# Layer 1's value rows in seven buffers, gate reads tied to a tile six ahead, and the last norm's weights read near the end

## The chip, the cores and the metric

The kernel runs on one core of one Trainium2 chip. The metric is the device time of one execution, in microseconds (us). It is given as a median of several executions, and separately for one profiled execution, whose trace is what is read below. A TensorE matmul is written PE, its weight load PEld; DVE is VectorE, ACT is ScalarE, POOL is GpSimd, SP is SyncE. SP, ACT and POOL also issue the transfers (DMA); "ACTq" and "SPq" in a row mean that issuing side.

## The reference

Two layers are applied to 256 tokens of width 1024 (and, in layer 0 alone, to 256 context tokens). Each layer has a mixer (a convolution, a neighbourhood attention and a grouped attention) and then a feed-forward part with 16384 experts (PEER). The change touches the feed-forward part:

```python
q = (xc @ w_q).reshape(PEER_CHUNK, PEER_HEADS, 2, PEER_D_KEY)
s = jnp.einsum('chpk,hpnk->chpn', q, sub_keys).astype(jnp.float32)
top_s, top_i = lax.top_k(s, PEER_TOPK)
...
g = jax.nn.softmax(best_s, axis=-1).astype(xc.dtype)
act = jax.nn.gelu(jnp.einsum('cd,chkd->chk', xc, jnp.take(u, idx, axis=0)))
return jnp.einsum('chk,chkd->cd', g * act, jnp.take(v, idx, axis=0))
```

Each token picks 16 experts for each of 8 heads; `u` and `v` hold one row of 1024 numbers per expert. At the very end the tokens go through one more root-mean-square norm with the weights `final_norm_g`.

## The kernel before

Most tokens are not gathered but computed against all experts. The 16384 experts of a layer are 128 tiles of 128. For a tile `e` the activations of its experts for all dense tokens are one product with `u` (helper `act`, the matmul of layer 1 is L630, those of layer 0 go through L119 to L121), they are multiplied by a gate that is zero for experts that a token did not pick (L827), and the result is multiplied with the tile's value rows `v` and summed in PSUM over all tiles (`down_proj`: L119 to L121 with the value rows split into a high and a low half, and in layer 1 also L842 on the unsplit rows). A few tokens go the other way: their rows are gathered with indirect transfers (L926) and worked on by DVE (L914, L921). These gathers are spread over the tiles by `gather_steps`.

`route` works out the gates and writes them to DRAM (`gd`), 128 x 128 x 16 numbers for each group of 16 tokens. `sweep` then goes over the tiles in order. It reads gates for 8 tiles at a time into `gr` (two buffers, transfers issued by ACT, L825); in layer 1 the gates of tiles 0 to 7 never leave the chip (`near`). 32 activation tiles of layer 1 (42 of layer 0) are computed while `route` still runs and are kept in DRAM (`spilled`); the sweep reads them back in pairs (`gback`, L719, issued by ACT). 8 more in layer 1 (4 in layer 0) wait in buffers. So in layer 1 the sweep's first 40 tiles need no new activations, while later ones need one 512 KB read of `u` and one of `v` per tile, both issued by SP (L109). `u` has a ring of three buffers (`rawu`), and so has `v` (`rawv`). A value buffer is free again when ACT has made the high half (L97), DVE the low half (L99) and PE has done its products with the raw rows (L842).

The order of the instructions on each engine is fixed before the run, by a planner that goes by a model of times, by data and buffers, and by the edges that `hold` adds (the first argument may not start before the second has ended). On the chip each engine, and each issuing queue, works strictly in that order. The list `los` holds, for each tile, the DVE instruction that ends the preparation of its gated activations (L832). Tiles are prepared up to two ahead of PE, since `whi` and `wlo` have two buffers.

In layer 1 the buffers `hiu` and `lou` (two each, 4 KB per partition, as large as a value tile) hold the split halves of the query weights before the sweep; the sweep itself does not use them, because layer 1 multiplies with unsplit `u`.

Of the kernel before, what the change touches and what calls it, by code (L numbers as in the profile page):

```python
# [11 lines left out]
F32 = mybir.dt.float32  # L12
# [9 lines left out]
P = 128  # L22
T = 256
D = 1024
# [17 lines left out]
NE = 128  # L42
EG = 8
GA = {0: 4, 1: 8}
SPILL = {0: 42, 1: 32}
GLAG = 3
GB = 8
WOV = {0: (0, 1), 1: (1, 1)}
ZAT = (0, 2, 4, 6, 7, 9)
# [3 lines left out]
def hymba_kernel(ctx: ExitStack, tc: tile.TileContext, a, out):  # L53
    nc = tc.nc
# [4 lines left out]
    ring = ctx.enter_context(tc.tile_pool(name="ring", bufs=2))  # L59
# [3 lines left out]
    def bank(tag, nm):  # L63
        return psum.tile([P, 512], F32, tag=tag, name=nm)
# [21 lines left out]
    def hold(ins, after):  # L86

        if after is not None:
            tc.add_manual_dep(ins.ins, after.ins.name,
                              mybir.DependencyInfo(mybir.DependencyClass.Sync, mybir.DependencyReason.DATA),  # L90
                              reason="work that would crowd out more urgent work")


    def split(raw, shape, kind, nm, lo_eng=None, after=None):
        hi = ring.tile(shape, F32R, tag="hi" + kind, name="hi_" + nm)
        lo = ring.tile(shape, F32R, tag="lo" + kind, name="lo_" + nm)
        S.activation(hi, raw, AF.Copy)  # L97
        if lo_eng is None or lo_eng is V:
            V.tensor_tensor(lo, raw, hi.bitcast(F32), ALU.subtract)  # L99
        else:  # L100
            n = shape[1] // 4 if len(shape) == 3 and shape[1] == NC else 0
            for i in range(4):
                sl = (slice(None), slice(i * n, (i + 1) * n)) if n else (slice(None), i // 2, slice((i % 2) * 256, (i % 2 + 1) * 256))
                hold(lo_eng.tensor_tensor(lo[sl], raw[sl], hi[sl].bitcast(F32), ALU.subtract), after)  # L104
        return hi, lo

    def load(src, shape, kind, nm):
        raw = ring.tile(shape, F32, tag="raw" + kind, name="raw_" + nm, bufs=3)
        nc.sync.dma_start(raw, src)  # L109
        return raw  # L110
# [479 lines left out]
    def peer(l):  # L590
# [120 lines left out]
        def act_of(e, sw, after):  # L711
# [5 lines left out]
            if i % 2 == 0:  # L717
                two[0] = sw.tile([P, 2, nd], F32, tag="gback", name=f"gback{l}_{e}", bufs=GB // 2)
                hold(nc.scalar.dma_start(two[0], spilled[:, i:i + 2, :]), after)  # L719
# [89 lines left out]
    def sweep(l, dense, gath, act, h2n, eidx, gates, gd, nd, nb):  # L809
        sw = ctx_peer.enter_context(tc.tile_pool(name=f"sw{l}", bufs=2))  # L810
        pair = l == DEPTH - 1
        nw = P if pair else nd
        acc = [[bank(f"x{j}", f"acc{l}{j}{h}") for h in range(1 if pair and j else 2)] for j in range(len(dense))]
        steps = gather_steps(l, gath or [1], h2n, eidx, gates, sw, H if pair else P)
        ng = len(steps)
        ahead = GA[l] + SPILL[l]
        gr = None
        rows = None
        last = []
        los = []  # L820
        for e in range(NE):
            ga = act(e, sw, los[(e - GA[l]) // 2] if 0 <= e - GA[l] < GB else None)
            if e % EG == 0 and e >= NEAR[l]:
                gr = sw.tile([P, nb, EG, TB], F32, tag="gr", name=f"gr{l}_{e}")
                nc.scalar.dma_start(gr, gd[1][:, :, e:e + EG, :])  # L825
            g = gr[:, :, e % EG, :] if e >= NEAR[l] else gd[0][:, :, e, :]
            wi = V.tensor_tensor(ga[:, :nd].rearrange("p (b t) -> p b t", t=TB),  # L827
                            ga[:, :nd].rearrange("p (b t) -> p b t", t=TB), g, ALU.mult)
            whi = sw.tile([P, nw], F32R, tag="whi", name=f"whi{l}_{e}")
            wlo = sw.tile([P, nw], F32R, tag="wlo", name=f"wlo{l}_{e}")  # L830
            S.activation(whi, ga[:, :nw], AF.Copy)  # L831
            los.append(V.tensor_tensor(wlo, ga[:, :nw], whi.bitcast(F32), ALU.subtract))  # L832
            if e >= 2:
                hold(wi, los[e - 2])
            raw = load(a["v"][l, e], [P, D], "v", f"v{l}_{e}")
            v = split(raw, [P, D], "v", f"v{l}_{e}")

            def down_proj(j, h, e=e, whi=whi, wlo=wlo, v=v, ga=ga, raw=raw):
                ts, hs = slice(j * P, (j + 1) * P), slice(h * 512, (h + 1) * 512)
                if pair and j:  # L840

                    return [PE.matmul(acc[1][0][k * H:(k + 1) * H], lhsT=ga[:, P:P + H], rhs=raw[:, k * 512:(k + 1) * 512],  # L842
                                      start=e == 0, stop=e == NE - 1) for k in range(2)]
                return mm3(acc[j][h], whi[:, ts], wlo[:, ts], v[0][:, hs], v[1][:, hs], e == 0, e == NE - 1)

            if e < NE - 2:
                for j in range(len(dense)):
                    for h in range(len(acc[j])):
                        down_proj(j, h)
            else:  # L850
                last.append(down_proj)
            while steps and (e >= NE - 2 or ng - len(steps) < ng * (4 * e - 3 * min(e, ahead)) // (480 - 3 * ahead)):
                steps.pop(0)(wi)
            if e == NE - 12:
                rows = gate_rows(l, 5, [0, 1] if gath else [0], "mm")
            if e == NE - 2 and not pair:
                for g, t in enumerate(gath):
                    V.tensor_tensor(h2n[g], h2n[g], rows[t // 2], ALU.mult)
                    V.tensor_tensor(resid[t], resid[t], h2n[g], ALU.add)
                    for h in range(2):  # L860
                        squares(t, h)
        assert not steps
        if l == DEPTH - 1:
            fg = sw.tile([P, D], F32, name="fg", bufs=1)
            nc.scalar.dma_start(fg, a["fin_g"].partition_broadcast(P))
            V.tensor_scalar(fg, fg, 32.0, None, op0=ALU.mult)

        prev = None
        for j, h, e in LORD[l]:
            if e is None:  # L870

                accs = sw.tile([P, 512], F32, tag="ap", name="accs", bufs=3)
                S.activation(accs, acc[1][0], AF.Copy)
                acc[1] = [bank("x2", f"accj{k}") for k in range(2)]
                ins = []
                for k in range(2):
                    ins += [PE.matmul(acc[1][k][:H], lhsT=ident[:, k * H:(k + 1) * H], rhs=accs, start=True, stop=True),
                            PE.matmul(acc[1][k][H:], lhsT=fold, rhs=h2n[0][:, k * 512:(k + 1) * 512], start=True, stop=True)]
            else:
                ins = last[e](j, h)  # L880
            for i in ins:
                hold(i, prev)
                prev = i
        for j, t in [(1, 1), (0, 0)] if pair else enumerate(dense):
            for h in range(2):
                residual(sw, t, h, acc[j][h], rows, norm_ins["h10"][0] if len(dense) == 3 and j == 2 else None)
            if len(dense) == 3 and j == 1:
                norm_rs["h10"] = inv_rms(cst, [0, 1], "h10")
            if l == DEPTH - 1:
                y = sw.tile([P, D], F32, tag="grow", name=f"y{t}", bufs=GLAG + 1)  # L890
                y = [y[:, :512], y[:, 512:]]
                G.tensor_tensor(y[1], resid[t][:, 512:], fg[:, 512:], ALU.mult)
                rs = inv_rms(sw, [t], f"f{t}")
                V.scalar_tensor_tensor(y[0], resid[t][:, :512], rs, fg[:, :512], op0=ALU.mult, op1=ALU.mult)
                S.activation(y[1], y[1], AF.Copy, scale=rs)
                for h in range(2):
                    nc.sync.dma_start(out[t * P:(t + 1) * P, h * 512:(h + 1) * 512], y[h])

    def gather_steps(l, gath, h2n, eidx, gates, sw, ns):
# [5 lines left out]
        def use(after):  # L905
            rows, f = waiting.pop(0)
            hold(f(rows), after)

        for g in range(len(gath)):
# [13 lines left out]
            def step(k, after, g=g, t=t, down=down, up=up):  # L923
                s = k % ns
                r = sw.tile([P, D], F32, tag="grow", name=f"gr{'uv'[k // ns]}{l}{t}{s}", bufs=GLAG + 1)
                d = G.indirect_dma_start(out=r, out_offset=None, in_=a["v_rows" if k >= ns else "u_rows"],  # L926
                                         in_offset=bass.IndirectOffsetOnAxis(ap=eidx[g][:, s:s + 1], axis=0))
                hold(d, after)
                waiting.append((r, lambda rows, s=s, f=up if k >= ns else down: f(s, rows)))
                if len(waiting) > GLAG:  # L930
                    use(after)
# [3 lines left out]
        if steps:  # L935
            steps.extend([use] * GLAG)
        return steps
# [89 lines left out]
```

## Time and profile before

| | us |
|---|---|
| median of 3 executions | 2615.96 (2612.59 to 2622.68) |
| the profiled execution | 2629.2 |
| its span in the trace | 2627.1 |
| PE busy in the span | 2491.1 (95%) |
| DVE busy | 1831.6 (70%) |
| ACT busy | 1052.3 (40%) |
| POOL busy | 1050.9 (40%) |

The trace begins with the span; 2.1 us of the profiled execution lie outside of it. A matmul counts as busy while it is in the pipeline, so PE's share says little about its pace; the pace is read from the times between starts. "Granted clock" is the share of TensorE's full clock that it was given: of its two levels, 1.0 stands for 2.4 GHz and 0.5 for 1.2 GHz, and a value between is a mean over a stretch. The sweep of layer 0 begins at about 700 us of the span, that of layer 1 at about 2008 us, and the last tile of layer 1 ends at about 2612 us.

### The profile page before, as it was taken

The numbers are of one execution on the slowest core, as the hardware profiler recorded it, in microseconds if no ns is written. First come the engines' busy times: TensorE is split into PE (matmuls) and PEld (weight loads), VectorE is DVE, ScalarE is ACT, GpSimd is POOL, SyncE is SP. The second block draws the span as 40 slices with busy tenths as digits, with TensorE's granted clock in tenths as the row PEclk, the third lists the DMA queues.
The fourth block names the chain that finished last, engine by engine and source line by source line (L and its number), as shares of the span: only waits on it lengthen the run. The fifth ranks groups of instructions, "written<-read, shape, count | busy, mean of one in ns | idle before, by whom it ended". The sixth has DMA issues, their size and how long they took to land. (4 is left out here: it accounts for less than half of the span.)

```text
span 2627.1 us, 38186 instructions
## 1 busy us (share of the span) xinstructions
PE 2491.1 (95%) x13837; PEld 2023.0 (77%) x13837; DVE 1831.6 (70%) x3506; ACT 1052.3 (40%) x1708; POOL 1050.9 (40%) x967
## 2 busy tenths in 40 slices
PE   7999999888899999999999998998998999999997
PEld 4755788877898888989989987855997756777775
DVE  1754589989546677787888885374994467666667
ACT  3345633367533333333333334445454333323323
POOL 3713434768642244454545441722600114223222
PEclk9999999999999999999999999998999999999999
DMA  7343364356878889999999992441579889999996
GB/s 270 104 169 122 127 245 145 119 211 263 311 257 276 293 295 328 326 343 339 347 331 342 338 336 85 161 164 49 159 241 344 278 286 326 377 356 361 350 366 234
DMA packets 263565, 681.42 MB, mean 259 GB/s; under 512 B 23840, under 2 KB 112976, under 8 KB 260304
## 3 DMA queue, kind: packets, MB, share of 16 engines
q1 hardware_dynamic: 121712, 423.48, 45.4%
q0 software_dynamic: 55296, 201.35, 20.8%
q10 hardware_dynamic: 86368, 54.15, 7.2%
q8 instruction: 109, 1.79, 0.3%
q14 instruction: 80, 0.66, 0.1%
HBM read 628.63 MB, written 49.44 MB: 258 GB/s over the span
## 5 line engine op out<-in xcount | busy, mean ns | idle before, releaser
L120 PE MATMUL acc<-lo_v,whi 128*128 128x512 f32 x1024 | 406.1, 397 | 2.9 <-DVE lo_v L99 2.8
L99 DVE TENSOR_TENSOR lo_v<-raw_v,hi_v 128x1024 fp32r<-128x1024 f32 x256 | 313.5, 1225 | 119.9 <-ACT hi_v L97 119.1
L630 PE MATMUL psu<-h2raw,raw_u 128*128 128x192 f32 x2048 | 364.9, 330 | 10.1 <-DMA raw_u<-in_u 6.3
L121 PE MATMUL acc<-hi_v,wlo 128*128 128x512 f32 x1024 | 374.4, 392 | 0.0
L97 ACT ACTIVATE hi_v<-raw_v 128x1024 fp32r<-128x1024 f32 x256 | 269.1, 1052 | 260.4 <-PE acc L121 234.5
L630 PEld LDWEIGHTS psu<-h2raw,raw_u 128*128 128x128 f32 x2048 | 339.8, 191 | 40.2 <-issue 20.7
L121 PE MATMUL psu<-ahi_m,lo_u 128*128 128x384 f32 x1024 | 351.7, 343 | 10.2 <-DVE lo_u L99 6.6
L119 PE MATMUL psu<-ahi_m,hi_u 128*128 128x384 f32 x1024 | 349.9, 342 | 7.0 <-ACT hi_u L97 2.9
L120 PE MATMUL psu<-alo_m,hi_u 128*128 128x384 f32 x1024 | 349.8, 342 | 0.0
L119 PE MATMUL acc<-hi_v,whi 128*128 128x512 f32 x1024 | 346.2, 404 | 2.9 <-ACT hi_v L97 2.7
L926 POOL DMA_INDIRECT gru<-in_u_rows,eidx x128 | 183.6, 1435 | 286.3 <-DVE gback L827 144.8
L119 PEld LDWEIGHTS acc<-hi_v,whi 128*128 128x128 f32 x1024 | 184.9, 188 | 104.1 <-ACT gact L633 55.2
L921 DVE SCALAR_TENSOR_TENSOR h2n<-grv,dots,h2n 128x1024 f32<-128x1024 f32 x190 | 243.0, 1279 | 26.0 <-DMA grv<-in_v,eidx 24.6
L914 DVE SCALAR_TENSOR_TENSOR gru<-gru,h2n 128x1024 f32<-128x1024 f32 x192 | 232.0, 1220 | 36.7 <-DMA gru<-in_u_rows,eidx 31.8
L104 POOL TENSOR_TENSOR lo_u<-raw_u,hi_u 128x256 fp32r<-128x256 f32 x184 | 213.1, 1190 | 95.2 <-ACT hi_u L97 84.0
L926 POOL DMA_INDIRECT grv<-in_v,eidx x128 | 171.3, 1338 | 188.3 <-DVE h2n L921 164.3
L926 POOL DMA_INDIRECT gru<-in_u_rows,egl x64 | 90.2, 1409 | 376.3 <-DMA spilled<-gsp 123.2
L120 PEld LDWEIGHTS acc<-lo_v,whi 128*128 128x128 f32 x1024 | 192.6, 188 | 55.8 <-issue 5.7
L121 PEld LDWEIGHTS acc<-hi_v,wlo 128*128 128x128 f32 x1024 | 192.3, 188 | 38.1 <-DVE wlo L832 0.3
L831 ACT ACTIVATE whi<-gact 128x128 fp32r<-128x128 f32 (+1 forms) x182 | 74.6, 410 | 337.2 <-PE acc L120 189.8
L121 PEld LDWEIGHTS psu<-ahi_m,lo_u 128*128 128x128 f32 x1024 | 195.7, 191 | 16.9 <-DVE lo_u L99 8.6
L119 PEld LDWEIGHTS psu<-ahi_m,hi_u 128*128 128x128 f32 x1024 | 195.8, 191 | 13.1 <-ACT gsp L633 3.5
(287 smaller groups left out, 4581.3 us busy)
## 6 DMA issues: line engine op xcount, KB each, us to landing
raw_u<-in_u SPq DMA_DIRECT2D x256, 512.0 KB, 5.6
raw_v<-in_v SPq DMA_DIRECT2D x256, 512.0 KB, 6.0
ada<-in_ada SPq DMA_DIRECT2D x96, 512.0 KB, 4.7
gd<-stage SPq DMA_DIRECT2D x24, 1024.0 KB, 5.5
gr<-gd ACTq DMA_DIRECT2D x16, 1536.0 KB, 25.2
raw_wq<-in_w_q SPq DMA_DIRECT2D x32, 512.0 KB, 3.6
raw_wout<-in_w_out SPq DMA_DIRECT2D x24, 512.0 KB, 3.5
gd<-stage SPq DMA_DIRECT2D x12, 960.0 KB, 5.8
```

The source lines that it names most:

```text
L97: S.activation(hi, raw, AF.Copy)
L99: V.tensor_tensor(lo, raw, hi.bitcast(F32), ALU.subtract)
L104: hold(lo_eng.tensor_tensor(lo[sl], raw[sl], hi[sl].bitcast(F32), ALU.subtract), after)
L119: return [PE.matmul(o, lhsT=ahi, rhs=bhi, start=first, stop=False), PE.matmul(o, lhsT=ahi, rhs=blo, start=False, stop=False), PE.matmul(o, ...
L120: PE.matmul(o, lhsT=ahi, rhs=blo, start=False, stop=False),
L121: PE.matmul(o, lhsT=alo, rhs=bhi, start=False, stop=last)]
L630: PE.matmul(ps[:, :nd], lhsT=u[:, c, :], rhs=h2raw[:, c, :nd], start=c == 0, stop=c == NC - 1)
L831: S.activation(whi, ga[:, :nw], AF.Copy)
L914: return V.scalar_tensor_tensor(r, r, 1.0, h2n[g], op0=ALU.mult, op1=ALU.mult, accum_out=dots[:, s:s + 1])
L921: return V.scalar_tensor_tensor(h2n[g], r, dots[:, s:s + 1], h2n[g], op0=ALU.mult, op1=ALU.add)
L926: d = G.indirect_dma_start(out=r, out_offset=None, in_=a["v_rows" if k >= ns else "u_rows"], in_offset=bass.IndirectOffsetOnAxis(ap=eidx[g ...
```

## The change

There are three edits, all in `sweep`.

```diff
+GRL = 6
+VRING = (("hiu", 2), ("lou", 2), ("rawv", 3), ("hiu", 2), ("lou", 2), ("rawv", 3), ("rawv", 3))
...
                 gr = sw.tile([P, nb, EG, TB], F32, tag="gr", name=f"gr{l}_{e}")
-                nc.scalar.dma_start(gr, gd[1][:, :, e:e + EG, :])
+                hold(nc.scalar.dma_start(gr, gd[1][:, :, e:e + EG, :]), los[e - GRL] if e >= GRL else None)
...
-            raw = load(a["v"][l, e], [P, D], "v", f"v{l}_{e}")
+            if pair:
+
+                tag, bufs = VRING[e % len(VRING)]
+                raw = ring.tile([P, D], F32, tag=tag, name=f"raw_v{l}_{e}", bufs=bufs)
+                nc.sync.dma_start(raw, a["v"][l, e])
+            else:
+                raw = load(a["v"][l, e], [P, D], "v", f"v{l}_{e}")
...
             fg = sw.tile([P, D], F32, name="fg", bufs=1)
-            nc.scalar.dma_start(fg, a["fin_g"].partition_broadcast(P))
+            hold(nc.scalar.dma_start(fg, a["fin_g"].partition_broadcast(P)), los[NE - 16])
```

In layer 1 (`pair`) the value rows of seven tiles in a row now go into seven buffers: two `hiu`, two `lou` and three `rawv`. In both layers the gate read of a block of 8 tiles that begins at tile `e` may start only when the gated activations of tile `e - 6` are ready; before, it could start as soon as one of the two `gr` buffers was free, that is, when the last gates of the block two earlier had been used (tile `e - 9`), and the first two reads at once. The read of the final norm's weights (512 KB in SBUF) may start only when the activations of tile 112 of layer 1 are ready. No instruction of arithmetic is added or removed, and the same bytes are read.

## Rows read from the trace of the kernel before

**Rows 1.** Stages of layer 1's sweep: from and to, length, then busy us of PE, PEld, DVE, ACT and POOL (number of instructions), granted clock, share of the DMA engines' time, GB/s. All in us from the span's start.

```profile
2008.00:2140.00 132.00, 128.99 (x589) 86.95 (x588) 57.23 (x99) 40.95 (x74) 16.44 (x10) 0.97 0.87 290
2140.00:2182.00 42.00, 36.28 (x141) 18.30 (x140) 32.28 (x54) 17.54 (x29) 12.79 (x7) 0.96 0.86 294
2182.00:2240.00 58.00, 56.21 (x269) 40.01 (x268) 40.32 (x70) 17.95 (x33) 26.56 (x17) 1.00 0.93 340
2240.00:2560.00 320.00, 320.00 (x1606) 240.35 (x1606) 212.91 (x304) 99.07 (x188) 95.92 (x82) 1.00 0.98 361
2588.00:2610.00 22.00, 20.60 (x86) 10.45 (x84) 21.17 (x28) 10.21 (x16) 7.18 (x4) 1.00 0.70 261
```

**Rows 2.** The chain of work that ended last, from 2080 us to the end: shares by engine and line, and three neighbouring pieces of it (start, us, what, number of records).

```profile
by line: PE psu L630 40.7%; PE acc L842 19.2%; PE acc L119 10.8%; PE acc L120 9.0%; PE acc L121 8.5%; DMA raw_v<-in_v 4.0%; issue 2.2%; DVE lo_v L99 0.8%; ACT hi_v L97 0.8%; DVE res L572 0.6%; DVE h2n L921 0.5%; DVE dres L571 0.5%; DVE wlo 
...
2401.22 2.60 PE psu L630 x16
2403.82 1.01 PE acc L842 x4
2406.41 2.60 PE psu L630 x16
```

**Rows 3.** Records of one line of the kernel in stretches of the sweep (from and to, length, busy us, number of records, granted clock, DMA share, GB/s): the first two rows are L842, four records per tile, the last two L630, sixteen records per tile.

```profile
2008.00:2240.00 232.00, 62.34 (x212) 0.98 0.89 303
2140.00:2180.00 40.00, 14.91 (x52) 0.96 0.85 292
...
2008.00:2240.00 232.00, 87.19 (x465) 0.98 0.89 303
2240.00:2588.00 348.00, 185.01 (x1072) 1.00 0.98 358
```

**Rows 4.** The beginning of layer 0's sweep: ACT's instructions and its issuing side in order of time (start, us, what, idle time before and what ended it), one PE row, and the stage from 700 to 720 us with the columns of rows 1.

```profile
696.97 9.49 ACTq L825 DMA_DIRECT2D gr<-gd  x2
706.58 0.49 ACT L633 ACTIVATE gsp<-psu 128x384 f32<-128x384 f32 x1 [8.29 <-issue]
706.97 2.00 ACT L97 ACTIVATE hi_u<-raw_u 128x1024 fp32r<-128x1024 f32 x2
...
708.08 0.69 PE L119 MATMUL psu<-ahi_m,hi_u 128*128 128x384 f32 x1 [2.90 <-ACT hi_u L97]
...
700.00:720.00 20.00, 17.10 (x80) 16.39 (x80) 5.01 (x6) 4.45 (x8) 9.42 (x12) 0.83 1.06 323
```

**Rows 5.** The beginning of layer 1's sweep, ACT and its issuing side, then PE.

```profile
2008.82 2.33 ACTq L825 DMA_DIRECT2D gr<-gd  x2
2011.24 8.84 ACTq L719 DMA_DIRECT2D gback<-spilled  x1
2020.66 1.06 ACT L97 ACTIVATE hi_v<-raw_v 128x1024 fp32r<-128x1024 f32 x1 [0.15 <-issue]
2020.69 0.36 ACTq L865 DMA_DIRECT2D fg<-in_fin_g  x1
...
2013.91 5.47 PE L630 MATMUL psu<-h2raw,raw_u 128*128 128x192 f32 x32
2021.77 0.79 PE L119 MATMUL acc<-hi_v,whi 128*128 128x512 f32 x1 [2.40 <-ACT hi_v L97]
```

**Rows 6.** The stretch of layer 1's sweep in which tiles need no activations: SP's issues, the time from issue to landing of these value reads, and two PE rows.

```profile
2141.31 41.09 SPq L109 DMA_DIRECT2D raw_v<-in_v  x14
...
DMA to landing us min/median/max: 3.6/5.8/9.5
...
2149.33 1.08 PE L842 MATMUL acc<-raw_v,gback 128*64 128x512 f32 x4 [2.42 <-DMA raw_v<-in_v]
2174.98 3.49 PE L842 MATMUL acc<-raw_v,gact 128*64 128x512 f32 x8 [2.36 <-DMA raw_v<-in_v]
```

**Rows 7.** Gate reads (`gr`), time from issue to landing: all 15 of layer 1; the one issued at 2143 us; those of layer 0 between 690 and 900 us. Then the issue of two neighbouring reads of layer 0, for blocks of 8 tiles each.

```profile
DMA to landing us min/median/max: 8.2/13.1/29.8
DMA to landing us min/median/max: 12.7/12.7/12.7
DMA to landing us min/median/max: 14.5/17.7/18.5
...
762.84 0.54 ACTq L825 DMA_DIRECT2D gr<-gd  x1
...
802.46 0.53 ACTq L825 DMA_DIRECT2D gr<-gd  x1
```

**Rows 8.** Two neighbouring issues of SP in layer 1's sweep, and the PE row that follows.

```profile
2215.74 0.33 SPq L109 DMA_DIRECT2D raw_v<-in_v  x1
2229.59 0.33 SPq L109 DMA_DIRECT2D raw_u<-in_u  x1
...
2234.37 2.87 PE L630 MATMUL psu<-h2raw,raw_u 128*128 128x192 f32 x16 [1.69 <-DMA raw_u<-in_u]
```

**Rows 9.** The stage from 1890 to 1900 us, before layer 1's sweep, with the columns of rows 1; all transfers from 2008 to 2610 us; the reads of `u` between 2250 and 2550 us (number, KB each, median us from issue to landing).

```profile
1890.00:1900.00 10.00, 10.00 (x67) 10.00 (x66) 10.00 (x72) 4.07 (x8) 0.00 (x0) 1.00 0.40 124
...
DMA packets 77037, 200.64 MB, mean 333 GB/s; under 512 B 6219, under 2 KB 32083, under 8 KB 76996
...
raw_u<-in_u SPq DMA_DIRECT2D x58, 512.0 KB, 6.1
```

**Rows 10.** One group of the page's costliest instructions: line, engine, operation, shapes, number, then busy us and mean ns of one, then idle time before.

```profile
L921 DVE SCALAR_TENSOR_TENSOR h2n<-grv,dots,h2n 128x1024 f32<-128x1024 f32 x190 | 243.0, 1279 | 26.0 <-DMA grv<-in_v,eidx 24.6
```

## The prediction, written before the result was known

> **What bounds the kernel now.** I read the stages of layer 1's sweep first. From 2240 to 2560 us PE is busy without a gap while the DMA engines are at 0.98 [rows 1]; the chain of waits from 2080 us on lies mostly on PE, with 4.0% on value reads [rows 2]. So the next question is whether PE or the transfers set the pace of a tile. Neighbouring starts in the chain give the answer: the `u` product takes 2.60 us, and the next one starts 5.19 us after the last [rows 2], so a tile that needs no new activation takes 5.19 - 2.60 = 2.59 us of PE. The count of records checks it: 1072/16 = 67 `u` products from 2240 to 2588 us, 67 x 5.19 = 348 us, the length of the stretch [rows 3]. PE waits for nothing there, and no edit shortens its work.
>
> Before 2240 us the same count leaves something over. From 2008 to 2240 us there are 212/4 = 53 tiles and 465/16 = 29.1 `u` products [rows 3]: 53 x 2.59 + 29.1 x 2.60 = 212.9 of 232 us, so PE loses 19.1 us. That, one stall in layer 0 of the same look, and the last tiles are all that the change can win.
>
> **Part 1: the second gate read leaves the start of layer 0.** ACT issues two gate reads in a row at 696.97 us, which hold its issuing side for 9.49 us; its next work idles 8.29 us with "issue" as the reason, and PE waits 2.90 us for the high half of `u` behind it [rows 4]. Later single reads cost about 0.53 us to issue [rows 7]. In the new kernel the second read waits for tile 2, so the block of ACT should go. PE wins the 2.90 us and what the clock took afterwards: the granted clock is 0.83 from 700 to 720 us [rows 4], which between its two levels 1.0 and 0.5 is 20 x 0.17/0.5 = 6.8 us at half pace, 3.4 us lost. Bounds 0 (the `u` read is late by itself) to 6.3 us; I take 5.5, near the top, because the idle ACT is the nearer row. What is late next is the first gate read itself, which the sweep needs anyway.
>
> **Part 2: the start of layer 1.** It looks the same: two gate reads at 2008.82, then a `gback` issue that takes 8.84 us, the high half of a value tile only at 2020.66, and PE, done with 32 records of `u` at 2013.91 + 5.47 = 2019.4, idles 2.40 us [rows 5]. The clock is 0.97 of 132 us [rows 1]: 132 x 0.03/0.5 = 7.9 us at half pace, 4.0 us lost. With the gate reads tied to tiles 2 and 10, the final norm's read (issued at 2020.69, rows 5) gone, and tiles 3 to 6 in buffers that need not wait for tile 0, I take 6 of these 6.4 us; bounds 0 to 11 (the 19.1 us less parts 3 and 4).
>
> **Part 3: seven value buffers in the bare tiles.** From 2140 to 2180 us there are 52/4 = 13 tiles [rows 3], 33.7 us of work in 40: 6.3 us lost. SP issues 14 value reads in a row there, 41.09/14 = 2.9 us apart, each landing after 5.8 us (median, up to 9.5), and PE waits 2.42 and 2.36 us for them by name [rows 6]. Three buffers cover at most 3 x 2.59 = 7.8 us of landing, splitting and release; seven cover 18.1 us, above the worst landing. The four added reads are 4 x 0.524 = 2.1 MB, early; DMA is at 0.86 here [rows 1], so room is there. I take 5; bounds 0 to 6.3.
>
> **Part 4: the rest up to 2240 us.** PE is idle 58 - 56.2 = 1.8 us in the last 58 us [rows 1]. SP stands still from 2215.74 to 2229.59 and PE then waits 1.69 us for a `u` read [rows 8]; value reads were held up in the same queue. The deeper ring covers the value side only. I take 2; bounds 0 to 6.4 (19.1 - 6.4 - 6.3).
>
> **Part 5: what the gate reads' new wait may cost.** The read sits on ACT's queue until tile `e-6` is ready; behind it wait the next Gelu, `whi` and `hi_v`, and PE for these. The awaited DVE instruction directly needs the `whi` just ahead, so the planner can hardly place the read early; I count this as nothing, with a bound of 3 x 1.28 = 3.8 us per badly placed read from the DVE instructions that may lie between (1.28 us each for the longest) [rows 10]. The lead matters more. In bare tiles six tiles are 6 x 2.59 = 15.5 us; the read of 2143 us landed after 12.7, but landings reach 29.8 us [rows 7]. Two blocks (32 and 40) lie there: 0 to 2 x 14.3 = 28.6 us; I take 2 by the row of that very stretch, with a little for busier queues. Where `u` is also read the lead is 6 x 5.19 = 31.1 us, above every landing: 0. In layer 0, 8 tiles take 802.46 - 762.84 = 39.6 us, so the lead is 29.7 us against 14.5 to 18.5 [rows 7]: 0.
>
> **Part 6: the small ones.** The first value reads of layer 1 can go out when the query weights are done, at about 1890 us, where DMA is at 0.40 [rows 9]: 0, with 2 us as a bound if they push `u` reads back. The final norm's read, 0.524 MB at 361 GB/s [rows 1], is 1.45 us of transfer in a stretch at 0.98: 0 to 1.45, I take 0, since PE waits for nothing there. Its DVE scaling may fall between the last tiles, where DVE is busy 21.2 of 22 us [rows 1]; that stage is DVE's, so the deeper ring wins nothing in it either.
>
> **Sum.** -5.5 - 6 - 5 - 2 + 2 = -16.5 us against the profiled execution's 2629.2 (span 2627.1 and 2.1 around it). That execution lies 13.2 us above the median 2615.96, with the same stalls assumed in both, so the forecast is 2615.96 - 16.5 = 2599.5 us.
>
> **Rivals.**
> A: the ring does not do what it says. SP is one queue in the planner's order; if the value reads stay behind `u` reads that wait for PE, four more buffers stay empty. For it: SP's stop at 2215.74. Against it: in rows 6 only value reads stand in line. Then parts 3 and 4 fall away, part 2 keeps its ACT share of 4: -9.5, or 2606 us.
> B: the transfers take it back. After the bare tiles up to four more value reads stand in line before each `u` read, 4 x 1.45 = 5.8 us; a `u` read that lands in 6.1 us [rows 9] would take 11.9, while two tiles of cover are 10.4. The loss ends when the backlog is worked off, so at most 5.8 us: -16.5 + 5.8 = -10.7, or 2605 us. For it: 0.98 in rows 1; against it: 200.64 MB [rows 9] at 361 GB/s need 556 us of the 602, so the sweep as a whole is not short of transfers.
> The Trainium skill ("DMA: Bandwidth & Descriptors", section Specifications) gives about 358 GB/s as one core's share of HBM. By that, the steady tile's 361 x 5.19 = 1.87 MB would need 5.23 us, an estimate, and the 67 tiles would come 3 us later than B has it. The trace disagrees: 361 GB/s over 320 us with PE never waiting [rows 1].
> C, slower: late gates. If the bare tiles run faster, DMA fills up, and the two gate reads of blocks 32 and 40 land as slowly as the slowest of rows 7 (29.8 us). DVE then stands at L827 with all the splits behind it: +28.6, parts 3 and 4 gone, parts 1 and 2 kept (-11.5): 2633 us. The turn lies at a landing of 15.5 + 11.5/2 = 21.2 us. For it: the slowest landings are those with DMA above 0.9. Against it: the bare stretch itself showed 12.7.
>
> **How the numbers follow.** Forecast 0.58, A 0.17, B 0.13, C 0.12. The forecast's own range is 2590 (all upper bounds: 6.3 + 19.1) to 2609. Half a per cent, 13 us, is about what can be told from no change here: 2603 and 2629. Of the forecast three quarters lie below 2603 (0.43), of A and B a sixth (0.05): faster 0.48. Slower is most of C: 0.10. The rest, 0.42, is the same. The range with 8 in 10 reaches from 2588 to 2620; what it leaves out is C and a little below.
>
> **What would show it.** Part 1: no idle "issue" of 8 us on ACT near 700 us, granted clock near 1.0 from 700 to 720. Part 2: no issue of 8.84 us after 2008, PE without the 2.40 us gap. Part 3: value reads issued up to seven tiles ahead and none named as PE's releaser between the 26th and 40th tile; 13 bare tiles in about 34 us. Part 5: no DVE idle ended by `gr` in layer 1. Part 6: DMA above 0.5 near 1890 us. The prediction is wrong if the sweeps' PE idle time stays at 19 us, if DVE waits for gates, or if `u` reads take over as PE's releaser after tile 40.

## The result, and the profile after

The changed kernel takes 2632.0 us (2626.4 to 2636.6, nine runs) beside 2616.0 us before (2610.2 to 2623.6, nine runs): 16 us more by the medians, and some 14 by the ratio of 1.0055 [1.004, 1.007], where 2599.5 was forecast. Its profiled execution took 2629.05 us, span 2627.2, as good as equal to the profiled execution of before, which lies 13 us above its own median. So the two traces are compared place by place, not by their ends, and a second trace of before (below) stands beside them.

What was to be won before 2240 us is there. ACT's rows at the start of layer 0 (start, us, what, idle time before), and the stage from 700 to 720 us with the columns of rows 1:

```profile
694.17 0.59 ACTq L827 DMA_DIRECT2D gr<-gd  x1
711.23 0.52 ACT L833 ACTIVATE whi<-gact 128x384 fp32r<-128x384 f32 x1 [7.41 <-DVE gact L829]
...
700.00:720.00 20.00, 18.90 (x102) 17.54 (x101) 6.03 (x9) 6.73 (x10) 11.89 (x15) 1.00 0.80 265
```

One gate read, 0.59 us of ACT's issuing side instead of 9.49, and a granted clock of 1.00 instead of 0.83 [rows 4]; ACT still idles 7.41 us, but now for DVE's gate product. Layer 1, stages as in rows 1; then the records of the half-width value products (L850, four a tile) and of the `u` products (L632, sixteen each) as in rows 3 (a line's number shifts a little from kernel to kernel; these were L842 and L630):

```profile
2008.00:2140.00 132.00, 132.00 (x572) 82.45 (x572) 67.51 (x111) 43.49 (x76) 18.95 (x11) 1.00 0.84 279
2140.00:2182.00 42.00, 41.08 (x174) 24.13 (x174) 32.11 (x56) 16.14 (x28) 16.78 (x11) 1.00 0.98 355
2182.00:2240.00 58.00, 58.00 (x258) 37.42 (x256) 41.35 (x71) 21.07 (x37) 21.14 (x15) 1.00 0.95 341
2240.00:2560.00 320.00, 307.09 (x1501) 226.40 (x1499) 202.26 (x288) 96.37 (x175) 99.14 (x84) 0.99 0.95 349
...
2008.00:2240.00 232.00, 75.03 (x232) 1.00 0.89 308
2240.00:2588.00 348.00, 72.11 (x250) 0.99 0.94 345
...
2008.00:2240.00 232.00, 83.54 (x432) 1.00 0.89 308
2240.00:2588.00 348.00, 174.37 (x999) 0.99 0.94 345
```

By the prediction's own count, 58 tiles and 27 `u` products before 2240 us are 220.4 of 232 us: 11.6 us lost, where before lost 19.1. PE's waits there sum to 0.9 us, none for a value row. After 2240 us comes what the forecast ruled out: 62.5 tiles and 62.4 `u` products are 324 of 348 us, 24 us lost in the stretch where before lost nothing [rows 3]. Of these, 15.0 are named waits, 3.4 a lower clock, and most of the rest four split pairs, as shown below. The wait table of that stretch (who waited for what, us, times, longest), rows of PE around one wait, rows of ACT and DVE during it, and PE's clock after it (columns as in rows 1):

```profile
PE acc L850 <- DVE gact L829: 15.0, 13, 2.1
...
2425.78 0.59 PE L632 MATMUL psu<-h2raw,raw_u 128*128 128x192 f32 x2
2428.47 1.98 PE L850 MATMUL acc<-raw_v,gact 128*64 128x512 f32 x4 [2.09 <-DVE gact L829]
2430.37 0.80 PE L121 MATMUL acc<-hi_v,whi 128*128 128x512 f32 x1
...
2426.41 0.33 ACT L635 ACTIVATE gact<-psu 128x192 f32<-128x192 f32 x1 [0.47 <-PE psu L632]
2426.92 1.22 DVE L101 TENSOR_TENSOR lo_v<-raw_v,hi_v 128x1024 fp32r<-128x1024 f32 x1
2428.06 0.35 DVE L829 TENSOR_TENSOR gact<-gact,gr 128x192 f32<-128x192 f32 x1
...
2428.00:2430.00 2.00, 1.53 (x4) 0.51 1.01 397
2430.00:2432.00 2.00, 2.00 (x6) 0.50 0.83 287
2432.00:2434.00 2.00, 2.00 (x7) 0.50 0.82 262
2434.00:2436.00 2.00, 2.00 (x11) 0.78 0.63 236
```

PE ends a `u` product, and the next in its order is a product with the activation made from just such a product: it stands for the Gelu and DVE's gate product. Three of the 13 waits are 0.81 us, where DVE was free; here DVE was first busy with the split of a value row (1.22 us), and PE stood 2.09. After this wait the granted clock was 0.50 (the lower level, 1.2 GHz) for 6.8 us (three of the windows and 0.9 us of the fourth), which cost PE 3.4; the four records took 1.98 us instead of 1.08. No other stretch of this sweep is at the lower level.

The split pairs are seen only in the starts of neighbouring PE rows. First the changed kernel, then the kernel before with a tie in layer 0 alone (an experiment below):

```profile
2095.59 1.07 PE L850 MATMUL acc<-raw_v,gback 128*64 128x512 f32 x2
2096.59 0.73 PE L121 MATMUL acc<-hi_v,whi 128*128 128x512 f32 x2
2097.26 1.07 PE L850 MATMUL acc<-raw_v,gback 128*64 128x512 f32 x2
2098.26 0.59 PE L632 MATMUL psu<-h2raw,raw_u 128*128 128x192 f32 x2
```

```profile
2097.17 1.08 PE L850 MATMUL acc<-raw_v,gback 128*64 128x512 f32 x4
2098.18 1.08 PE L632 MATMUL psu<-h2raw,raw_u 128*128 128x192 f32 x5
```

The two half-width products of a tile write rows 0 to 63 and 64 to 127 of one accumulator. Next to each other they take 1.01 us together (2097.17 to 2098.18). With other work between, each takes 1.00 us (2095.59 to 2096.59, 2097.26 to 2098.26): a split pair costs up to 1 us, and no wait shows it. Of the 19 that PE's order has in this sweep, 15 lie before 2240 us and 4 behind. The Trainium skill ("TensorEngine Tiling (Array Packing)", section Key Properties) says that different tiles of the array can run their products in parallel. The trace agrees, with one condition more: only where the two are neighbours in the order.

### The profile page after: what moved, and what is told of

It is laid out like the page before. It is cut to its first block, busy times and chain, and to the rows that moved or that the text cites. A ratio compares the mean times of both kernels' runs of the same rounds, so it can differ in the third digit from the quotient of the medians.

```text
span 2627.2 us, 38165 instructions
## 1 busy us (share of the span) xinstructions
PE 2502.7 (95%) x13837; PEld 2024.8 (77%) x13837; DVE 1824.5 (69%) x3506; ACT 1060.5 (40%) x1710; POOL 1043.9 (40%) x967
## 4 chain that ended last, share of the span: by engine, by line
PE 67%; DVE 12%; issue 8%; DMA 4%; POOL 4%; ACT 2%; DVEq 0%; ACTq 0%; POOLq 0%; SPq 0%
PE psu L632 12%; PE acc L121 6%; PE acc L122 6%; PE acc L123 6%; PE acc L850 5%; PE psu L123 4%; PE psu L121 4%; PE psu L122 4%; POOL gru L934 3%; PE psada L223 2%; PE psq L121 1%; DVE ohC L796 1%; DVE ohA L796 1%; DVE ohB L793 1%; PE psq L122 1%
## 5 line engine op out<-in xcount | busy, mean ns | idle before, releaser
L632 PEld LDWEIGHTS psu<-h2raw,raw_u 128*128 128x128 f32 x2048 | 339.7, 192 | 55.1 <-issue 38.8
L632 PE MATMUL psu<-h2raw,raw_u 128*128 128x192 f32 x2048 | 369.4, 332 | 9.5 <-DMA raw_u<-in_u 4.8
L121 PE MATMUL acc<-hi_v,whi 128*128 128x512 f32 x1024 | 358.5, 406 | 1.1 <-ACT whi L833 1.1
L934 POOL DMA_INDIRECT grv<-in_v,eidx x128 | 165.4, 1292 | 191.3 <-DVE h2n L929 159.6
L122 PEld LDWEIGHTS psu<-alo_m,hi_u 128*128 128x128 f32 x1024 | 196.0, 191 | 3.7
```

The costliest lines, as they stand in the source:

```text
L121: return [PE.matmul(o, lhsT=ahi, rhs=bhi, start=first, stop=False), PE.matmul(o, lhsT=ahi, rhs=blo, start=False, stop=False), PE.matmul(o, ...
L122: PE.matmul(o, lhsT=ahi, rhs=blo, start=False, stop=False),
L632: PE.matmul(ps[:, :nd], lhsT=u[:, c, :], rhs=h2raw[:, c, :nd], start=c == 0, stop=c == NC - 1)
```

## The experiments

In the table, "split pairs" and "in reserve" (activations done but not yet used, in the steady stretch) are of PE's planned order, which is fixed before a run. The ratio is to the kernel before on the same chip, whose median was 2616 to 2619 us each time.

| kernel | ring | ties L0, L1 | in reserve | split pairs | us | ratio |
|---|---|---|---|---|---|---|
| before | no | - | 7 | 4 | 2616.0 | |
| before_again | no | - | 7 | 4 | 2621.2 | 1.0008 [0.9989, 1.0027] |
| changed kernel | yes | both | 0 to 1 | 19 | 2632.0 | 1.0055 [1.004, 1.007] |
| ring_only | yes | - | 0 to 1 | 23 | 2638.1 | 1.0080 [1.0061, 1.0099] |
| gates_only | no | both | 8 | 8 | 2630.0 | 1.0055 [1.0036, 1.0073] |
| gates_l0 | no | L0 | 7 | 4 | 2609.0 | 0.9970 [0.9950, 0.9989] |
| gates_l1 | no | L1 | 8 | 8 | 2631.1 | 1.0051 [1.0035, 1.0067] |
| gates_far | no | both, 12 in L1 | 7 | 7 | 2622.1 | 1.0013 [0.9996, 1.0029] |
| ring40 | to tile 39 | both | 6 | 12 | 2619.8 | 1.0014 [0.9994, 1.0034] |
| after_res6 | yes | both | 6 | 16 | 2616.1 | 0.9989 [0.9973, 1.0006] |
| after_res1 | yes | both | 1 | 20 | 2622.5 | 1.0015 [1.0002, 1.0028] |
| before_cap2 | no | - | 1 | 2 | 2618.5 | 0.9997 [0.9978, 1.0017] |
| before_cap1 | no | - | 0 | 2 | 2617.0 | 0.9994 [0.9978, 1.0009] |
| after_pair | yes | both | 0 to 1 | 1 | 2631.3 | 1.0058 [1.0035, 1.0081] |
| gates_l0_pair | no | L0 | 8 to 9 | 1 | 2626.7 | 1.0032 [1.0017, 1.0046] |
| l0_pair_cap8 | no | L0 | 6 to 7 | 1 | 2635.3 | 1.0092 [1.0057, 1.0127] |
| res6_nogate | yes | - | 6 | 17 | 2624.1 | 1.0016 [1.0002, 1.0030] |
| res6_pair | yes | both | 6 | 1 | 2608.1 | 0.9973 [0.9955, 0.9991] |
| res6_l0_pair | yes | L0 | 6 | 0 | 2605.9 | 0.9948 [0.9928, 0.9968] |
| res7_l0_pair | yes | L0 | 7 | 0 | 2603.2 | 0.9944 [0.9925, 0.9963] |

### One part at a time

ring_only (against the changed kernel; the final norm's read loses its edge too):
```diff
-hold(nc.scalar.dma_start(gr, gd[1][:, :, e:e + EG, :]), los[e - GRL] if e >= GRL else None)
+nc.scalar.dma_start(gr, gd[1][:, :, e:e + EG, :])
```


> The ring of seven value buffers alone; the gate reads and the final norm's read start as in the kernel before. Theory R (reserve): with value rows early the planned order of PE takes tiles first and lets the reserve of ready activations run down from 7 tiles to about 0 by tile 60; from then on PE waits in each tile for Gelu and the gate product. Then this kernel keeps the whole loss and lacks what the gate reads win: 2628 to 2645 us, and PE's waits for DVE at L827's counterpart of 20 us and more after 2240 us stay. Theory G (late gates): the loss comes from the gate reads' new wait, so this kernel is faster than before, 2600 to 2612 us.

gates_only (the ties, with the old buffers and the old read of the final norm's weights):
```diff
-            if pair:
+            if False:
```


> The gate reads tied six tiles ahead alone; three value buffers and the final norm's read as before. Theory R: the planned order keeps a reserve of 8 activations, the starts of both sweeps win up to 11 us: 2604 to 2612 us. Theory G: slower than before, 2625 to 2635 us, with DVE idle at the gate product until a gate read lands.

The ring alone costs 20 us, the ties alone 12, and both together not 32 but 14: they don't add, since each makes the planner write another order. Of theory R the time of ring_only held (its waits after 2240 us are 11.0 us, though, not 20 and more), its claim for the ties didn't. Theory G was right on gates_only, where DVE waits 18.2 us for gates in layer 1, and wrong on ring_only. In the next two the tie of gates_only holds in one layer only (`l == 0`, gates_l0, or `l == 1`, gates_l1):

gates_l0:

> The kernel before with the tie on gate reads in layer 0 alone (old three value buffers, final norm's weights read where they were, layer 1's gate reads free; its planned order of layer 1 on TensorE is that of the kernel before, 7 activations in reserve). The run with ties in both layers took 2630.0 beside 2617.7 of before, and no theory has explained its 12 us yet. Theory A (the 12 us come from layer 0: gates that land late there hold up products): 2627 to 2633. Theory B (they come from layer 1, by the order that the tie makes the planner choose, 8 in reserve, which is all the buffers there are): 2610 to 2619, with layer 0's first value products at 712 to 716 us.

gates_l1:

> The kernel before with the tie on gate reads in layer 1 alone (layer 1's planned order on TensorE is that of the run with both ties, 8 activations in reserve). Theory A (the 12 us of the two ties come from layer 0): 2614 to 2620, as before. Theory B (from layer 1): 2627 to 2633. If the profile shows products of layer 1 waiting for VectorE's gate product and that for a landing of gr, it is the late gate itself; if it shows waits on split value rows or on buffers, it is the changed order.

Theory B held, gates_l0 one microsecond below its range. The tie in layer 0 gains 8 us (0.5% less at best, 0.1% at least), the one in layer 1 costs 14. PE's waits in layer 0, the second trace of before and then gates_l0:

```profile
PE psu L121 <- DVE lo_u L99: 5.3, 4, 2.0
```

```profile
PE psu L123 <- DVE lo_u L101: 0.6, 1, 0.6
```

The first value products came at 720.1 us, though, not at 712 to 716 as expected. That is no sign against a gain at the start, for the first gate read was itself issued later there. That read and the first value product, in gates_l0 and then in the second trace of before:

```profile
703.75 0.59 ACTq L827 DMA_DIRECT2D gr<-gd  x1
720.12 0.39 PE L121 MATMUL acc<-hi_v,whi 128*128 128x512 f32 x1
```

```profile
701.51 7.66 ACTq L825 DMA_DIRECT2D gr<-gd  x2
719.69 0.39 PE L119 MATMUL acc<-hi_v,whi 128*128 128x512 f32 x1
```

From the issue to the product it is 16.4 us with the tie and 18.2 without. Over all traces of this document it is 16.4 to 20.3 us with the tie in layer 0 (13 traces, mean 17.8), and 18.2 to 24.8 without (7 traces, mean 22.2): the start gains 4.4 us in the mean. Layer 1's first value product, counted from that same issue, comes 7.0 us earlier in the mean. In gates_l1 the gate read is late; a DVE row and the PE row behind it:

```profile
2199.15 0.36 DVE L829 TENSOR_TENSOR gact<-gact,gr 128x192 f32<-128x192 f32 x1 [8.35 <-DMA gr<-gd]
...
2200.70 0.80 PE L122 MATMUL acc<-lo_v,whi 128*128 128x512 f32 x1 [4.83 <-DVE lo_v L101]
```

DVE stands 8.35 us for the read of gates, the split of a value row waits behind it, and PE 4.83 us for that; 40 us later the same again with 3.44 us. With twelve tiles of lead in layer 1:

```diff
-hold(nc.scalar.dma_start(gr, gd[1][:, :, e:e + EG, :]), los[e - GRL] if e >= GRL else None)
+hold(nc.scalar.dma_start(gr, gd[1][:, :, e:e + EG, :]), (los[e - GRL] if e >= GRL else None) if l == 0 else (los[e - 12] if e >= 12 else None))
```

gates_far:

> The kernel before with gate reads tied six tiles ahead in layer 0 and twelve ahead in layer 1 (old three buffers; planned: 7 split tiles instead of 8 with six ahead and 4 before, 7 activations in reserve instead of 8). Six ahead in layer 1 alone took 2631.1; there VectorE stood 22.6 us for landings of gr, 8.4 at the longest. Theory L (lateness: the read lands behind queued value rows, VectorE stands for it, and the split value row behind it comes late to TensorE): no such wait here, 2609 to 2615. Theory O (any tie in layer 1 gives a poorer order): 2622 to 2632.

DVE no longer waits for gates in layer 1, and 9 us come back, but 2622 is still 13 above gates_l0. Lateness is part of the price; the rest goes with the order (7 split pairs, and PE waits for rows of `v` and `u`; the table of sweeps below has both kernels).

before_again:

> The kernel before, unchanged, for a second profile of it. The first profile's run took 2629.2, 13 us above the median. Theory S (those 13 us were stalls of that one run, and the forecast took away from the median what only this run had lost): the time is that of before, 2611 to 2624; layer 0's first value products come at 711 to 716 us (719.5 in the first profile), its value sweep lasts 900 to 903 us (908.6), layer 1's starts at 1994 to 2000 (2008.1). Rival (the stalls are in every run, and the other runs save elsewhere): the starts again at 718 to 721 and 2004 to 2010.

It took 2621.2 us, profiled span 2620.8. The stalls are there again, first value products at 719.7 us and layer 1's at 2005.8. The rival held: the stalls that the forecast counted are in other runs too, at the start of layer 0 in all seven traces without the tie. Layer 1's first value product comes at 1998.3 to 2011.5 us in these seven, so a good part of the 13 us is spread that arises before layer 1's sweep.

### The reserve

Why is PE's order so different with the ring? In the planned order of before, the read of value row 64 stands behind that of `u` row 71, in the changed kernel behind that of `u` row 61: the planner fills the four new buffers at the cost of `u`, and of 58 tiles from 64 on, 9 have their first value product right behind their own `u` product. Two ways back: hold the value products of tile `e` (from 34 on) until the `u` product of tile `e + 6` is done, or give value rows seven buffers only up to tile 39.

```diff
+            if pair and ahead <= e + LA < NE:
+                pre[e + LA] = act(e + LA, sw, None)
...
-                        down_proj(j, h)
+                        for i in down_proj(j, h):
+                            hold(i, lastmm[e + LA] if pair and 40 <= e + LA < NE else None)
```

after_res6:

> The changed kernel, and on top of it PE may do a tile's value products only when the activation product six tiles ahead is done (from tile 40 on), so that a reserve of six is kept in the planned order. Theory R: the loss goes and what remains are the gains: 2592 to 2608 us, PE steady at 5.2 us a tile. Theory T (transfers): value reads issued early stand before the reads of u; then PE waits for u reads by name instead, and the time stays at 2622 to 2635 us.

```diff
-                tag, bufs = VRING[e % len(VRING)]
+                tag, bufs = VRING[e % len(VRING)] if e < 40 else ("rawv", 3)
```

ring40:

> The changed kernel, but only tiles 0 to 39 use the seven buffers; later tiles use three. The planned order then keeps a reserve of six. Theory R: 2592 to 2608 us. Theory T: also better than the changed kernel, since the deep ring is gone where u is read; so this run tells R and T apart only together with the run that forces the reserve. If it is no faster than before, the bare tiles were not worth what was counted for them.

They take 16 and 12 us off the changed kernel, so theory T falls, but theory R's gain over before fails to come. Next the reverse: before with its reserve cut (`e - 1` in before_cap1).

```diff
+                    if c == 0:
+                        hold(i, done.get(e - 2) if e >= 48 else None)
```

before_cap2:

> The kernel before with one edge more in layer 1: from tile 48 on, an activation product may start only after the value products of the tile two before its own, so that the planned order keeps 1 activation in reserve (7 before); old buffers, no ties, 2 split pairs. Theory R (a reserve of 0 to 1 makes each tile wait for product, Gelu, gate product and value product in series, whatever the buffers): 2630 to 2645, with TensorE's waits on VectorE's gate product and on the Gelu in 2240 to 2590 us, as in the changed kernel. Rival (the reserve is a symptom; what costs is the ring's order of reads): 2613 to 2622.

before_cap1:

> The kernel before with an activation product from tile 48 on held until the value products of the tile just before its own are done: planned reserve 0, old buffers, no ties, 2 split pairs, activation rows read in step with their value rows (0 ahead). Theory Z (with a reserve of 0 each tile waits in series for product, Gelu, gate product and value product; one tile of reserve is enough to hide it): 2630 to 2645, with waits on VectorE's gate product in 2240 to 2590 us. Theory U (what costs in the changed kernel is that activation rows are read three tiles behind their value rows): 2613 to 2622.

Both cost nothing: a small reserve is not the cause in itself, and theory Z falls as it was put. The wait table of before_cap1 from 2240 to 2590 us, and PE rows of it:

```profile
PE acc L845 <- DVE gact L830: 0.7, 1, 0.7
...
2404.56 2.76 PE L631 MATMUL psu<-h2raw,raw_u 128*128 128x192 f32 x16
2407.02 0.76 PE L120 MATMUL acc<-lo_v,whi 128*128 128x512 f32 x2
2407.62 0.62 PE L121 MATMUL acc<-hi_v,wlo 128*128 128x512 f32 x2
2408.17 1.08 PE L845 MATMUL acc<-raw_v,gact 128*64 128x512 f32 x4
```

Here other products stand between a `u` product and the product with its activation (from tile 50 on 1.15 us of work at the least by the starts in the trace, 1.6 in the median), and the one wait is 0.7 us. What costs is a `u` product with nothing between it and its use. The changed kernel with one tile of reserve (after_res1) has no such place:

> The changed kernel whole with a reserve of one activation held by hand from tile 40 on (six took 2616.1); 20 split pairs planned (19 in the changed kernel, 16 with six in reserve), activation rows still read three tiles behind their value rows. Theory Z: 2614 to 2622. Theory U: 2627 to 2636.

2622.5 is half a microsecond above Z's range and 4.5 below U's, so theory U falls too: 9.5 of after_res6's 16 us come back though `u` is still read three rows late. Its waits in the sweep fell from 15.9 to 3.6 us.

### The split pairs

One edge more on both half-width products (after_pair; `lead` is the tile's first product with the low half of its value row):

```diff
+                    for i in both:
+                        hold(i, lead.get((l, e)))
```


> The changed kernel with one edge more in layer 1: both half-width products of a tile (64 rows of the accumulator each) may start only after the first product of the tile with the low half of its value row, so that they stand next to each other in TensorE's planned order. In the traces so far such a pair takes 1.00 us when adjacent and 1.00 us for each half when other products stand between; the planned orders have 4 split tiles before, 19 after, and the products with raw value rows take 146.1 us of after's layer-1 sweep, 134.1 of the second trace of before. Here 1 split tile is planned; the reserve of activations still falls to 0. Theory P (the splits are a cost of their own, beside the lost reserve): 2617 to 2624, raw products 133 to 136 us. Theory R (the lost reserve sets the pace, and what the pairs give back is waited for elsewhere): 2628 to 2636, with TensorE's waits in the sweep up from 15.9 us by some 10.

The time and the growth of the waits are those of theory R; its cause is only a part, as shown below. For each kernel I split layer 1's sweep, from first to last value product, by the starts of neighbouring PE rows into time of half-width products, named waits, and the rest (us):

| kernel | sweep | half-width | waits | rest |
|---|---|---|---|---|
| before_again | 602.6 | 134.1 | 9.6 | 459.0 |
| gates_l1 | 616.8 | 139.3 | 13.8 | 463.7 |
| gates_far | 610.1 | 138.2 | 11.8 | 460.0 |
| changed kernel | 623.5 | 146.1 | 15.9 | 461.5 |
| after_pair | 625.9 | 131.7 | 27.6 | 466.6 |
| after_res1 | 609.1 | 146.6 | 3.6 | 458.9 |
| res6_nogate | 609.0 | 143.1 | 5.2 | 460.7 |
| res6_l0_pair | 593.0 | 129.7 | 4.2 | 459.1 |
| res7_l0_pair | 592.0 | 130.5 | 2.9 | 458.5 |

Against the second trace of before the changed kernel loses 12.0 us to split pairs, 6.3 to waits and 2.5 to the rest (where most of the cost of the lower clock lies); the tie in layer 1 alone (gates_l1) loses 5.2, 4.2 and 4.7. With the pairs mended alone, 14.4 us come back, 11.7 are waited for instead and the rest grows by 5.1. PE's waits of after_pair from 2240 to 2590 us, then a row of DVE and one of PE before that:

```profile
PE acc L121 <- ACT whi L834: 16.7, 13, 1.7
...
2186.66 0.36 DVE L830 TENSOR_TENSOR gact<-gact,gr 128x192 f32<-128x192 f32 x1 [10.56 <-DMA gr<-gd]
2188.21 0.79 PE L122 MATMUL acc<-lo_v,whi 128*128 128x512 f32 x1 [6.22 <-DVE lo_v L101]
```

The lost reserve took back little of it: the waits after 2240 us are 16.7 us beside 15.0 in the changed kernel. The largest new wait is a late gate read once more: DVE stands 10.56 us for it, and PE 6.22 for the split of a value row behind it. The reserve alone gave 2616.1 us and the pairs alone 2631.3; both together, with all else of the change as it was, give 2608.1 (res6_pair). With the ring, reserve and pairs, and the tie where it gains:

res6_nogate:

> Seven value buffers and the reserve of six activations held by hand from tile 40 on, without the ties on gate reads and on the final norm's weights. The same with the ties took 2616.1. Theory R+G (the ties cost their 12 us in this order too): 2601 to 2608, faster than before. Theory S (the ties cost only in the order with 8 in reserve, and the gains read from the one profile of before are not there in its usual run): 2613 to 2622.

res6_l0_pair:

> Seven value buffers, reserve of six activations, adjacent pairs (none split in the planned order), gate reads tied in layer 0 alone, the final norm's weights read where they were. Ring and reserve without ties took 2624.1, with 143.1 us of raw products (17 split tiles planned); the tie in layer 0 alone gave 8 us. Theory P (all three add): 2624 less 8 less 9, 2604 to 2610, the fastest so far or level with the 2609 of the tie alone. Rival (the transfers or the other engines take back what the pairs give): 2613 to 2619.

res6_pair:

> The changed kernel whole (ring, ties in both layers, final norm's weights late) with both repairs, the reserve of six and adjacent pairs. With ties in layer 0 alone and the weights early it took 2605.9. Theory L (the tie in layer 1 lands late and costs of its own): 2612 to 2620. Theory O (the tie in layer 1 cost only by the orders that the planner chose with it): 2602 to 2609.

res7_l0_pair:

> As the fastest run so far (ring, adjacent pairs, tie in layer 0; 2605.9) with seven activations in reserve instead of six. Theory R: six is enough to hide the series of product, Gelu and gate product, and seven leaves one buffer free: 2602 to 2609. Theory F sharper (one free buffer is too few): 2610 to 2620.

res6_nogate took 2624.1 us, 2 above S's range and far above R+G's: beside the second trace of before, waits are down by 4.4 and split pairs up by 9.0. The same buffers and reserve with the ties took 2616.1, so there the ties gain some 8 us, as much as the one in layer 0 gained alone. With the pairs mended and the tie in layer 0, res6_l0_pair is 13 us faster than before and res7_l0_pair 14: the version that beats both kernels. In res6_pair, the whole change with both repairs, the tie in layer 1 and the late read of the weights cost no more than the runs can tell: 2608.1 beside 2605.9 on another chip, and by the two ratios 6 us with an uncertainty of 7. The time lies in O's range, but a late gate still costs of its own: DVE waits 17.9 us for gates, and PE once 5.00 us behind it. PE's waits in res7_l0_pair from 2002 to 2234 us; from there to 2582 us it has none:

```profile
PE acc L123 <- DVE lo_v L102: 2.9, 1, 2.9
PE acc L122 <- DMA raw_u<-in_u: 1.9, 1, 1.9
```

The same pairs without the ring are dear:

gates_l0_pair:

> The kernel before with the gate tie in layer 0 alone (2609.0) and adjacent pairs in layer 1 (1 split tile planned instead of 4; 8 to 9 activations in reserve instead of 7). Theory P: 3 us for the pairs, 2604 to 2608. Rival B (8 in reserve fills the buffers and costs, as it may have with the ties in layer 1): 2614 to 2624.

l0_pair_cap8:

> The run of the tie in layer 0 and adjacent pairs (2626.7, 8 to 9 activations planned in reserve) with one edge more: from tile 48 on an activation product starts only after the value products of the tile eight before it, whose buffer its Gelu needs; planned reserve 6 to 7. Theory F (with 8 in reserve all eight buffers are full, the Gelu stands at the head of ScalarE for one, and the split of the next value row stands behind it): 2603 to 2611. Rival (the adjacent pairs cost without the ring): 2620 to 2630.

(The edge of l0_pair_cap8 is that of before_cap2 with `e - 8`.) Theory P fell, and the rival's cause (theory F) too: 2626.7 lies above both ranges, and with the reserve at 6 to 7 the time rose to 2635.3, again above both. PE's waits in the sweep of l0_pair_cap8, which sum to 21.8 us beside 9.9 in gates_l0 (the two largest):

```profile
PE acc L121 <- ACT hi_v L99: 15.1, 13, 3.0
PE acc L122 <- DVE lo_v L101: 6.7, 14, 0.5
```

PE waits for split value rows. A pair that stands behind the low-half product keeps its raw row longer, and with three buffers the next row would then come later; this reading was not tried by itself.

## Why the prediction was wrong

The step that failed stands in its first paragraph: from 2240 us on "PE waits for nothing there, and no edit shortens its work". True, but the edits could lengthen it, and every term of the sum left PE's and SP's orders as they were, without a reason. More buffers and new edges gave the planner another order: 19 split pairs instead of 4, and `u` products right ahead of their use. Parts 2 to 5 had layer 1's sweep 11 us shorter; it came out 20.9 us longer than in the second trace of before (12.0 split pairs, 6.3 waits, 2.5 the rest).

- Part 1 (-5.5). Right in mechanism and size: in gates_l0 the tie gave -8 [-13, -3], the block of ACT is gone in all 13 traces with the tie, and the start is 4.4 us shorter in the mean.
- The 19.1 us from which parts 2 to 4 are taken. In that stretch PE's wait table of before sums to 10.4 us and the lower clock cost 5.1; the rest is mostly before's own four split pairs, which no buffer could win back.
- Parts 2 to 4 (-13). Half came: 7.5 us less lost by 2240 us (6.6 when counted from each sweep's first value product, 2008.1 and 1991.4 us), PE's 2.40 us gap and the waits for value rows gone. The rest went into 15 split pairs in the same stretch. Part 3's mechanism was right: no wait of PE in that stretch of the changed kernel is for a value row's transfer.
- Part 5 (+2). In the changed kernel DVE waited 3.7 us for gates in layer 1 and PE none of it, so the term was 0 there; with the old buffers DVE waited 22.6 us and PE some 8 behind it (gates_l1).
- Part 6 (0). The norm's weights were issued at 2527.4 us and scaled at 2542.7, far from the end; no run tried this edit alone.
- Rivals. A fell (the value reads did run ahead), B too: the DMA share fell to 0.95 from 0.98, and no `u` read held PE after 2240 us. C named the right sign and nearly the time (2633), but that was luck, for the cause was another: late gates hold PE for some 8 us in gates_l1, and not in the changed kernel. They do so again where the pairs are mended (6.22 us in after_pair, 5.00 in res6_pair). C's sign, DMA above 0.9, told nothing: in the trace of before it is above 0.9 during the quick landings of layer 1's gate reads as well.

With the order mended, the sum nearly comes out: -16.5 was forecast, and res7_l0_pair gives 0.9944 [0.9925, 0.9963], -15 us [-20, -10]. In part that is luck: it is another kernel (two edges more, no tie in layer 1, the norm's weights read early), and of the 10.6 us by which its sweep of layer 1 is shorter than in the second trace of before, 3.6 lie in half-width products, which no part counted. Open stays why the planner's order is poorer with the tie in layer 1, and why mended pairs are so dear with three buffers.

## What to carry to other kernels

Where a planner writes the order, a new buffer or edge is also a new order: count, before and after, how many pairs that ran side by side are split, how far each product stands ahead of its use, and which read stands ahead of which. Give the planner an edge for each of these properties together with the buffers, and measure each: the same edge for the pairs cost some 17 us where there were only three buffers. A busy engine without waits can still lose time: look at the distance between starts, not at busy time.

## What the runs showed of the hardware that I had not expected

Two products into different halves of the accumulator's rows take 1.01 us as neighbours and 1.00 us each when split. After a wait of 2.09 us PE's granted clock was at 0.50 for 6.8 us in one place of the changed kernel; at half pace that cost 3.4, more than the wait itself; in the second trace of before, all such stretches of the sweep sum to 3.4 us lost, so the clock makes no difference between the two kernels. ACT's issuing side was held 9.49 us by two neighbouring gate reads [rows 4] and 0.59 us by one; in the seven traces with two, the second alone held it for 7.0 to 11.8 us.
